# Five buffers for the later modulations' rows, and paired row chunks in the second product, of a two-layer decoder trunk

## The chip, the cores and the metric

One core of a Trainium2 chip runs the whole program. The metric is the device time of one execution in microseconds (us); the kernel before took 2310.33 us (median of three runs, 2307.93 to 2311.91). The engines are named as the profile names them: PE multiplies matrices, DVE (vector) and ACT (scalar) work on tiles, POOL (GpSimd) does a little arithmetic and issues transfers, SP only issues transfers. Each engine takes its instructions strictly in the order of the program.

## The reference

```python
for i in range(DEPTH):                       # 2 layers, D=2048, 256 tokens
    shift, scale, gate = ada_ln(c, mix_mod_w[i], mix_mod_b[i])   # silu(c) @ w + b, in three parts
    h = rms_norm(x, mix_norm_g[i]) * (1.0 + scale) + shift
    y = conformer_conv_module(h, ...) if i == 0 else stick_breaking_mixer(h, ...)
    x = x + gate * y
    shift, scale, gate = ada_ln(c, ffn_mod_w[i], ffn_mod_b[i])
    h = rms_norm(x, ffn_norm_g[i]) * (1.0 + scale) + shift
    x = x + gate * conv_ffn(h, ...)          # up to 2 x 5632, conv of width 3, silu(gate) * value, down
return rms_norm(x, final_norm_g)
```

`conformer_conv_module` is a first product `pw1` (to 2 x 2048), a gated depthwise convolution of width 31, a layer norm and a second product `pw2` (2048 to 2048). Every matrix is read once from HBM. Besides the weights there are four modulation matrices (`mix` and `ffn` of each layer) of 2048 x 6144, of which only the product with one vector, silu(c), is wanted.

## The kernel before

All activations lie transposed, in 16 tiles of 128 features by 256 tokens. A product takes its weights in blocks of 128 x 128, eight blocks (512 KB) to a piece. A piece is loaded into `raw` (SP's queue, L225, six buffers), split by ACT into a rounded part `wh` (L243) and by DVE into the rest `wl` (L247), four buffers of each. For every block PE runs three matmuls of 128 x 256: L297 (`wh` by the high part of the activation), L298 (`wh` by its low part), L299 (`wl` by the high part). Loads run five pieces ahead of PE and splits three.

The products follow each other on PE: `pw1`, `pw2`, then of the first ffn `up00a`, `up00b`, `up01a`, `down00`, `up01b`, `down01` (up and down in two halves each), attention, and the second ffn (`up10a` to `down11`). In the profile below `pw2` stands at 286.5 to 408.9 us, `up00b` at 433.1 to 658.0, `down00` at 669.2 to 793.3, `down01` at 1028.5 to 1163.5 and `down11` at 2175.7 to 2301.3. `down00`, `down01` and `down11` have 1056 matmuls each.

Whenever an output tile of `pw2` or of `down01` is complete, ACT or DVE adds it to the residual `x` (L942, L984), ACT squares it into `t` (L392), POOL adds the square to `sumsq` (L396), and ACT and DVE make the raw input of the next product from it (`hh` L448, `hl` L449).

The modulation vectors are made beside the products, in two ways:

- Row chunks. A 1 MB piece of the matrix is loaded with its input features on the partitions, and PE multiplies it by the vector `hot` in four matmuls of 128 x 512 (L576; each leaves two records). The bias columns of the conv module and the scale and half the shift of the first ffn come so. When a vector is complete, PE turns it (L592) and DVE adds the bias (L598). `load_rows` loads a chunk (L556, POOL's queue in `pw2`) as soon as its home is free: an `mraw` tile ("m") or, late, the one `zrow` tile ("z").
- Tiles. 1 MB with 128 outputs on the partitions is loaded into `mraw`, and DVE multiplies it by silu(c) and sums along the row (L330). Half of the first ffn's shift (eight tiles, `mod_part`, loaded on SP's queue among the weights) and all later vectors (112 tiles, `mods1`, loaded on POOL's queue by L323) come so. `mraw` has three buffers.

`mods0` and `mods1` are generators. After each piece a product adds its entry in `RATES` to a credit, and each whole credit advances the current generator by one step: one row chunk, or one tile loaded and, once more than two are ahead, the oldest one reduced. `behind(on)` keeps a tile's load behind the last POOL instruction written so far, and its reduction behind the last DVE instruction. The rest of the order on each engine is set by a scheduler.

Of the kernel before, what the change touches and what calls it, by code (L numbers as in the profile page):

```python
# [10 lines left out]
F32 = mybir.dt.float32  # L11
# [5 lines left out]
P = 128  # L17
# [14 lines left out]
MORE_ROWS = 4  # L32
SPLIT_ROWS = 3
# [2 lines left out]
ROWS_AT = {**{c: (11,) for c in (2, 4, 6, 8, 10, 12)}, 13: (16, 17), 14: (8, 12, 16), 15: (2, 13, 15, 17)}  # L36
ROWS_TAIL = 5

RATES = {"pw2": (1.0, 0.0), "up": (0.44, 0.25), "down": (0.5, 0.0), "qk": (0.3, 0.0), "v": (0.3, 0.0),
         "o": (0.45, -3.0), "up00a": (0.0, 0.0), "qk0a": (0.0, 0.0),  # L40
         "up00b": (0.44, -1.5), "up10a": (0.0, 0.0), "up10b": (0.25, -2.0), "v0": (0.0, 0.0), "qk0b": (0.3, -1.5)}
QUIET = 6
PRIORITY = 100


def plan(nbs, kts, first, stagger=4):
# [70 lines left out]
def hybrid_trunk(ctx: ExitStack, tc: tile.TileContext, cfg: Cfg, io: dict):  # L117
    nc = tc.nc
    D, T, H = cfg.D, cfg.T, cfg.H
    KD, KF, CW, FW = cfg.KD, cfg.KF, cfg.CW, cfg.FW  # L120
# [45 lines left out]
    cpar = {}  # L166
# [10 lines left out]
    fill = []  # L177
# [37 lines left out]
    def drain(gens):  # L215
        while gens:
            advance(gens, 1)
# [97 lines left out]
    macc = const.tile([P, 3 * KD], F32, name="macc")  # L315
    moda, have, shift_ready = {}, set(), {}

    def mod_load(m, nb, own=False):

        v = mpool.tile([P, D], F32, name="mraw")  # L320
        src = io["mt_" + m][mt_at[m].index(nb) if m in mt_at else nb]
        if own:
            nc.gpsimd.dma_start(v, src)  # L323
        else:
            load(src, v)
        return v

    def mod_reduce(m, nb, v):

        nc.vector.tensor_tensor_reduce(out=v, in0=v, in1=csr, scale=1.0, scalar=0.0, op0=ALU.mult, op1=ALU.add,  # L330
                                       accum_out=macc[:, nb:nb + 1])
# [11 lines left out]
    def mod_part(m, part, first):  # L343
        ahead = []
        for nb in range(part * KD + first, (part + 1) * KD):
            ahead.append((nb, mod_load(m, nb)))
            if len(ahead) > 1:
                mod_reduce(m, *ahead.pop(0))
            yield
        mod_reduce(m, *ahead.pop(0))  # L350
        mod_sum(m, part * KD + first, KD - first)
        yield

    later = []

# [139 lines left out]
    with ExitStack() as cv:  # L495
# [39 lines left out]
        def load_rows(most=1):  # L535

            while row_chunks and most:
                n = nrow["n"]
                near = n < nrow["near"]
                home = row_homes[n] if near else ("zmm"[n % 3] if n < 8 * KD // 4 else "zm"[n % 2]) if "z" in cpar else "m"  # L540
                cap = {"m": 3 if near else 1 + (n < 8 * KD // 4), "r": MORE_ROWS, "w": SPLIT_ROWS, "z": 1}[home]
                if sum(t[1] == home for t in row_tiles) >= cap:
                    break
                m, c, k0 = row_chunks.pop(0)
                src = io["mr_" + m][mr_at[m].index(c), :, k0 * 512:(k0 + 4) * 512]
                if home == "w":
                    v = [w_pool.tile([P, PW], F32R, name=x).bitcast(F32) for x in ("wh", "wl")]
                    for i in range(2):
                        load(src[:, i * PW:(i + 1) * PW], v[i])
                    v = [v[g // 2][:, g % 2 * 512:(g % 2 + 1) * 512] for g in range(4)]  # L550
                else:
                    v = (cpool2.tile([P, 4 * 512], F32, name="mrow", bufs=MORE_ROWS) if home == "r" else
                         cpar["z"].tile([P, 4 * 512], F32, name="zrow") if home == "z" else
                         mpool.tile([P, 4 * 512], F32, name="mraw"))
                    if "z" in cpar:
                        nc.gpsimd.dma_start(v, src)  # L556
                    else:
                        load(src, v)
                    v = [v[:, g * 512:(g + 1) * 512] for g in range(4)]
                row_tiles.append((v, home))  # L560
                nrow["n"] += 1
                most -= 1

        def mod_rows():

            for m, c0, n, done in rows_of:
                ps = (psum_acc if m == "ffn0" and c0 else psum_a)() if n else None  # L570
                for i in range(n):
                    for k0 in range(0, KD, 4):
                        v = row_tiles.pop(0)[0]
                        first, last = i == 0 and k0 == 0, i == n - 1 and k0 + 4 >= KD
                        for g in range(4):
                            nc.tensor.matmul(ps[32 * g:32 * g + 32, :], hot[:, k0 + g, 31 - i:63 - i],  # L576
                                             v[g], start=first, stop=last,
                                             tile_position=(0, 32 * g))
                        load_rows()
                        if later and nrow["bias"]:  # L580
                            later.pop(0)()
                        if last:
                            rows = cpool.tile([P, 512], F32, name="rows")
                            nc.scalar.copy(rows, ps)
                        else:
                            yield
                if n:
                    ps2 = psum_b()

                    def turn(rows=rows, n=n, ps2=ps2):  # L590
                        for b in range(4):
                            nc.tensor.matmul(ps2[:, b * n:(b + 1) * n], rows[:, b * P:(b + 1) * P], sel[:, :n],  # L592
                                             start=True, stop=True)

                    def bias(m=m, c0=c0, n=n, ps2=ps2, done=done):
                        o = modv[m][:, c0 * 4:(c0 + n) * 4].rearrange("p (c b) -> p b c", b=4)
                        v = pc(bname[m], c0 * 4, n * 4).rearrange("p (c b) -> p b c", b=4)
                        nc.vector.tensor_tensor(o, ps2[:, :4 * n].rearrange("p (b c) -> p b c", b=4), v, op=ALU.add)  # L598
                        done()

                    later.extend([turn, bias])
                    yield
            while later:
                later.pop(0)()
                yield

        def mods0():
            part = mod_part("ffn0", 0, 4 * cfg.rows0) if cfg.rows0 * 4 < KD else iter(())
            for _ in mod_rows():
                yield  # L610
                if ("ffn0", 1) in have and next(part, "end") != "end":
                    yield
            yield from part
            have.add(("ffn0", 0))

        gb = cpool.tile([P, KD], F32, name="gb")
        ready = {"k": 0}
        ys = [cpool.tile([P, T], F32, name=f"y{j}") for j in range(KD)]
        for kt in range(KD):
            nc.gpsimd.tensor_tensor(ys[kt], xs[kt], rs, op=ALU.mult)  # L620
        htiles = [h_tiles(kt) for kt in range(KD)]
# [328 lines left out]
    def ffn(i, entry, out):  # L950
        m = f"ffn{i}"
        NG = KF // 2 + 1
        with ExitStack() as fs:
            gpool = fs.enter_context(tc.tile_pool(name=f"g{i}", bufs=1))
            gh, gl = [None] * KF, [None] * KF
            pend = {}

# [24 lines left out]
            def down_done(h):  # L982
                def done(nb, ps):
                    nc.vector.scalar_tensor_tensor(xs[nb], ps[:, :T], gate(m, nb), xs[nb],  # L984
                                                   op0=ALU.mult, op1=ALU.add)
                    if h == 1 and i == 0:
                        out.add(nb)
                    elif h == 1:
                        out.add(xs[nb])
                        nc.scalar.activation(xs[nb], xs[nb], AF.Copy, scale=pc("fin_g", nb, 1))  # L990
                return done
# [6 lines left out]
            gemm(f"up{i}1b", hh, hl, up_done)  # L998
            act_tables("sqrt_and_others")
            gemm(f"down{i}1", gh, gl, down_done(1), quiet=QUIET)  # L1000

    def mods1():

        ahead = []

        def finish():
            m, part, nb, v = ahead.pop(0)
            on = last_of(nc.vector.engine)
            mod_reduce(m, nb, v)
            behind(on)  # L1010
            if nb + 1 == (part + 1) * KD:
                mod_sum(m, part * KD, KD)
                if part == 1:
                    mod_scale(m, 0, KD)
                have.add((m, part))

        for m, part in (("ffn0", 2), ("mix1", 1), ("mix1", 0), ("mix1", 2), ("ffn1", 1), ("ffn1", 0), ("ffn1", 2)):
            for nb in range(part * KD, (part + 1) * KD):
                on = last_of(nc.gpsimd.engine)
                ahead.append((m, part, nb, mod_load(m, nb, own=True)))  # L1020
                behind(on)
                if len(ahead) > 2:
                    finish()
                yield
        while ahead:
            finish()
            yield

    fill.append(mods1())
    entry1 = Entry("mix1")  # L1030
    ffn(0, entry, entry1)
# [268 lines left out]
```

## Time and profile before

| | |
|---|---|
| median of three runs | 2310.33 us (2307.93 to 2311.91) |
| the profiled execution | 2314.76 us, span 2313.1 us |
| mean granted clock of PE | 0.997 |
| busy: PE, DVE, ACT, POOL | 2273.3, 1737.9, 1163.5, 334.4 us |
| HBM read | 598.58 MB |

All times below are from the profiled execution, which is 4.43 us above the median of the runs. A busy PE is not a PE at its peak, since a matmul that waits inside the pipe counts as busy: stages are best compared by their length and the number of their matmuls. In a timeline row the bracket holds the idle time before the instruction and what ended it.

### The profile page before, as it was taken

What the parts mean: (1) busy time and instruction counts of PE and PEld (TensorE: products, weight loads), DVE (VectorE), ACT (ScalarE), POOL (GpSimd) and SP (SyncE); (2) the same over time, 40 slices, a digit from 0 to 9 for tenths busy, and PEclk for the clock granted to TensorE, in tenths of its full rate; (3) what the DMA queues carried; (4) which work ended last, traced back from release to release, by engine and by line L of the source; (5) the groups of instructions that cost most, each with busy time, mean ns of one, the idle gap of its engine ahead of it and who ended that gap; (6) DMA issues with size and microseconds to landing.
All of it is one profiled execution on the core that took longest, in us unless ns stands there. A gap on an engine that the chain in (4) does not pass through costs nothing.

```text
span 2313.1 us, 44241 instructions
## 1 busy us (share of the span) xinstructions
PE 2273.3 (98%) x17834; PEld 2170.2 (94%) x17834; DVE 1737.9 (75%) x2386; ACT 1163.5 (50%) x1776; POOL 334.4 (14%) x478
## 2 busy tenths in 40 slices
PE   7999999999999999999999999999999999999997
PEld 5888678999999999999999999999999999999997
DVE  7689968899998899998875555668666545666554
ACT  2056655755543355554465555647555434555543
POOL 4058713200001000001211000121000000000010
PEclk9999999999999999999999999999999999999999
DMA  9988798689999999998854555555555555555553
GB/s 394 417 323 308 272 370 350 236 319 362 344 362 386 361 343 358 348 357 329 330 182 164 165 172 174 164 191 177 189 191 186 189 187 187 190 186 190 188 186 110
DMA packets 139167, 603.56 MB, mean 261 GB/s; under 512 B 15441, under 2 KB 15569, under 8 KB 115153
## 3 DMA queue, kind: packets, MB, share of 16 engines
q1 hardware_dynamic: 120242, 464.42, 56.0%
q0 software_dynamic: 18720, 136.32, 15.8%
q8 instruction: 139, 2.28, 0.4%
q14 instruction: 66, 0.54, 0.1%
HBM read 598.58 MB, written 2.10 MB: 260 GB/s over the span
## 4 chain that ended last, share of the span: by engine, by line
PE 62%; issue 23%; DVE 5%; DMA 5%; POOL 2%; ACT 1%; POOLq 0%; SPq 0%; DVEq 0%; ACTq 0%
PE ps L297 17%; PE ps L298 17%; PE ps L299 16%; PE ps L663 5%; DMA mraw<-in_mt_mix 3%; POOL mraw L323 2%; DVE mraw L330 2%; DMA mraw<-in_mt_ffn 2%; DVE wl L247 1%; PE ps L1125 1%; PE ps L1127 1%; PE ps L1126 1%; PE ps L576 1%; PE auxa L576 1%; ACT hl L712 0%
## 5 line engine op out<-in xcount | busy, mean ns | idle before, releaser
L247 DVE TENSOR_TENSOR wl<-raw,wh 128x1024 fp32r<-128x1024 f32 x688 | 844.4, 1231 | 414.7 <-ACT wh L243 409.1
L243 ACT CAST wh<-raw 128x1024 fp32r<-128x1024 f32 x688 | 719.3, 1048 | 822.9 <-PE ps L298 645.9
L297 PE MATMUL ps<-hh,wh 128*128 128x256 f32 (+1 forms) x3264 | 915.8, 281 | 0.0
L298 PE MATMUL ps<-hl,wh 128*128 128x256 f32 (+1 forms) x3264 | 912.1, 279 | 0.0
L299 PE MATMUL ps<-hh,wl 128*128 128x256 f32 (+1 forms) x3264 | 908.3, 278 | 0.1
L298 PEld LDWEIGHTS ps<-hl,wh 128*128 128x128 f32 x3264 | 617.7, 189 | 0.3
L299 PEld LDWEIGHTS ps<-hh,wl 128*128 128x128 f32 x3264 | 612.8, 188 | 0.7 <-DVE wl L247 0.7
L297 PEld LDWEIGHTS ps<-hh,wh 128*128 128x128 f32 x3264 | 612.7, 188 | 0.3
L299 PE MATMUL ps<-gh,wl 128*128 128x256 f32 x1408 | 394.6, 280 | 7.1 <-DVE wl L247 7.1
L298 PE MATMUL ps<-gl,wh 128*128 128x256 f32 x1408 | 396.4, 282 | 0.0
L297 PE MATMUL ps<-gh,wh 128*128 128x256 f32 x1408 | 395.4, 281 | 0.0
L330 DVE CUSTOM_DVE_ANT_0 mraw<-mraw,csr 128x2048 f32<-128x2048 f32 x152 | 348.5, 2294 | 52.6 <-DMA mraw<-in_mt_mix 30.9
L299 PEld LDWEIGHTS ps<-gh,wl 128*128 128x128 f32 x1408 | 266.0, 189 | 8.1 <-DVE wl L247 8.1
L298 PEld LDWEIGHTS ps<-gl,wh 128*128 128x128 f32 x1408 | 266.9, 190 | 0.0
L297 PEld LDWEIGHTS ps<-gh,wh 128*128 128x128 f32 x1408 | 266.2, 189 | 0.0
L396 POOL TENSOR_TENSOR sumsq<-sumsq,t 128x256 f32<-128x256 f32 x56 | 65.0, 1162 | 885.8 <-ACT t L392 885.6
L663 PE MATMUL ps<-hh,raw 128*128 128x256 f32 x832 | 188.8, 382 | 0.0
L663 PEld LDWEIGHTS ps<-hh,raw 128*128 128x128 f32 x832 | 157.8, 191 | 28.3 <-issue 6.7
L964 DVE SCALAR_TENSOR_TENSOR t<-ps,par,t 128x254 f32<-128x254 f32 x328 | 157.1, 479 | 3.9
L703 DVE SCALAR_TENSOR_TENSOR auxb<-u,cpar,auxb 128x256 f32<-128x256 f32 x297 | 121.6, 483 | 4.5 <-ACT auxb L687 3.7
L838 POOL TENSOR_TENSOR y<-y,hl 128x256 f32<-128x256 f32 x143 | 104.4, 730 | 13.4 <-ACT hl L712 3.3
L961 ACT ACTIVATE t<-ps,par 128x256 f32<-128x256 f32 x164 | 91.8, 560 | 0.0
(247 smaller groups left out, 2271.3 us busy)
## 6 DMA issues: line engine op xcount, KB each, us to landing
raw<-in_w_down SPq DMA_DIRECT2D x176, 512.0 KB, 3.8
mraw<-in_mt_ffn POOLq DMA_DIRECT2D x64, 1024.0 KB, 8.3
raw<-in_w_pw SPq DMA_DIRECT2D x96, 512.0 KB, 7.9
mraw<-in_mt_mix POOLq DMA_DIRECT2D x48, 1024.0 KB, 8.1
raw<-in_w_up01b SPq DMA_DIRECT2D x84, 512.0 KB, 6.8
raw<-in_w_up11b SPq DMA_DIRECT2D x84, 512.0 KB, 3.5
raw<-in_w_up00b SPq DMA_DIRECT2D x80, 512.0 KB, 6.5
raw<-in_w_up10b SPq DMA_DIRECT2D x80, 512.0 KB, 3.5
```

What stands on the lines that cost most here:

```text
L243: nc.scalar.copy(wh[:, :n], v[:, :n])
L247: nc.vector.tensor_tensor(wl[:, :n], v[:, :n], wh[:, :n].bitcast(F32), op=ALU.subtract)
L297: nc.tensor.matmul(o, wh[:, c], xh[kt], start=first, stop=False, skip_group_check=halves > 0)
L298: nc.tensor.matmul(o, wh[:, c], xl[kt], start=False, stop=False, skip_group_check=halves > 0)
L299: nc.tensor.matmul(o, wl[:, c], xh[kt], start=False, stop=left[nb] == 0, skip_group_check=halves > 0)
L330: nc.vector.tensor_tensor_reduce(out=v, in0=v, in1=csr, scale=1.0, scalar=0.0, op0=ALU.mult, op1=ALU.add, accum_out=macc[:, nb:nb + 1])
L396: engine.tensor_tensor(self.sum, self.sum, sq, op=ALU.add)
L663: nc.tensor.matmul(banks[j][:, nb // KD * T:(nb // KD + 1) * T], w[:, b * P:(b + 1) * P], hf[kt], start=first, stop=left[j] == 0, skip_gro ...
L703: nc.vector.scalar_tensor_tensor(conv_ps[j], us[j % UBUFS][:, k:k + T], tap(j, k), conv_ps[j], op0=ALU.mult, op1=ALU.add)
L838: nc.gpsimd.tensor_tensor(ys[c], ys[c], pr, op=ALU.add)
L961: nc.scalar.activation(y, ps[:, :T], AF.Identity, bias=pc(f"fdb{i}", nb, 1), scale=w(FW - 1))
L964: nc.vector.scalar_tensor_tensor(y[:, s:], ps[:, :T - s], w(k), y[:, s:], op0=ALU.mult, op1=ALU.add)
```

## The change

The change has three parts. `mods1` gets a ring of five buffers, three `mraw` of the old pool and two of a new pool opened in the first ffn, and reduces a tile once five are ahead, so that four loads lead; the rate of `up00b` goes from 0.44 (credit from -1.5) to 0.45 (credit from 0), and what is left is drained at the end of the ffn. In `pw2` each step of `mods0` takes two row chunks, and their homes follow a written list, in which "y" stands for two tiles `yhalf` that before held the first product's sixteen `y` tiles and are dead by then; the caps on homes change to match. The eight tiles of the first ffn's shift go from SP's queue to POOL's, with two loads ahead in place of one.

```diff
+LATE_HOMES = "mmzyymmzyymzyyzyyzyy"
...
-         "up00b": (0.44, -1.5), "up10a": (0.0, 0.0), "up10b": (0.25, -2.0), "v0": (0.0, 0.0), "qk0b": (0.3, -1.5)}
+         "up00b": (0.45, 0.0), "up10a": (0.0, 0.0), "up10b": (0.25, -2.0), "v0": (0.0, 0.0), "qk0b": (0.3, -1.5)}
+MORE_MODS = 2
...
     def mod_part(m, part, first):
         ahead = []
         for nb in range(part * KD + first, (part + 1) * KD):
-            ahead.append((nb, mod_load(m, nb)))
-            if len(ahead) > 1:
+            ahead.append((nb, mod_load(m, nb, own=True)))
+            if len(ahead) > 2:
                 mod_reduce(m, *ahead.pop(0))
+                yield
+        while ahead:
+            mod_reduce(m, *ahead.pop(0))
             yield
-        mod_reduce(m, *ahead.pop(0))
         mod_sum(m, part * KD + first, KD - first)
...
-                home = row_homes[n] if near else ("zmm"[n % 3] if n < 8 * KD // 4 else "zm"[n % 2]) if "z" in cpar else "m"
-                cap = {"m": 3 if near else 1 + (n < 8 * KD // 4), "r": MORE_ROWS, "w": SPLIT_ROWS, "z": 1}[home]
+                home = row_homes[n] if near else LATE_HOMES[n - nrow["near"]] if "z" in cpar else "m"
+                cap = {"m": 3 if near else 2, "r": MORE_ROWS, "w": SPLIT_ROWS, "z": 1, "y": 2}[home]
...
+                         cpool.tile([P, 4 * 512], F32, name="yhalf", bufs=2) if home == "y" else
...
-                        load_rows()
+                        load_rows(2 if nrow["bias"] else 1)
...
         def mods0():
+
             part = mod_part("ffn0", 0, 4 * cfg.rows0) if cfg.rows0 * 4 < KD else iter(())
-            for _ in mod_rows():
+            rows = mod_rows()
+            while next(rows, "end") != "end":
+                if nrow["bias"]:
+                    next(rows, "end")
+                    yield
+                    for _ in range(2 if ("ffn0", 1) in have else 0):
+                        next(part, "end")
+                        yield
                 yield
-                if ("ffn0", 1) in have and next(part, "end") != "end":
-                    yield
-            yield from part
+            for _ in part:
+                yield
+                yield
             have.add(("ffn0", 0))
...
-        ys = [cpool.tile([P, T], F32, name=f"y{j}") for j in range(KD)]
+        yhalf = [cpool.tile([P, KD // 2 * T], F32, name="yhalf", bufs=2) for _ in range(2)]
+        ys = [yhalf[j * 2 // KD][:, j % (KD // 2) * T:(j % (KD // 2) + 1) * T] for j in range(KD)]
...
+            if i == 0:
+                more["pool"] = fs.enter_context(tc.tile_pool(name="mods", bufs=MORE_MODS))
...
             gemm(f"down{i}1", gh, gl, down_done(1), quiet=QUIET)
+            drain(fill)
 
     def mods1():
 
-        ahead = []
+        ahead, ring = [], [mpool] * 3 + [more["pool"]] * MORE_MODS
...
-                ahead.append((m, part, nb, mod_load(m, nb, own=True)))
+                ahead.append((m, part, nb, mod_load(m, nb, own=True, pool=ring[0])))
+                ring.append(ring.pop(0))
                 behind(on)
-                if len(ahead) > 2:
+                if len(ahead) == len(ring):
                     finish()
```

The first place is POOL in `pw2`. Before, the row chunks (`mr`, one matrix row piece each) go to `mraw` and `zrow` in turn:

```order
L556 DMA mraw<-in_mr_ffn 128x2048 x4
L556 DMA zrow<-in_mr_ffn 128x2048
L556 DMA mraw<-in_mr_ffn 128x2048 x2
L556 DMA zrow<-in_mr_ffn 128x2048
L556 DMA mraw<-in_mr_ffn 128x2048
L556 DMA zrow<-in_mr_ffn 128x2048
L556 DMA mraw<-in_mr_ffn 128x2048
L556 DMA zrow<-in_mr_ffn 128x2048
L396 TENSOR_TENSOR sumsq<-sumsq,t 128x256 x4
```

After the change, from the fifth chunk in `pw2` on (`mt` is a tile of the shift, which SP loaded before):

```order
L561 DMA yhalf<-in_mr_ffn 128x2048 x3
L561 DMA zrow<-in_mr_ffn 128x2048
L561 DMA yhalf<-in_mr_ffn 128x2048 x3
L561 DMA zrow<-in_mr_ffn 128x2048
L561 DMA yhalf<-in_mr_ffn 128x2048
L400 TENSOR_TENSOR sumsq<-sumsq,t 128x256
L561 DMA yhalf<-in_mr_ffn 128x2048
L400 TENSOR_TENSOR sumsq<-sumsq,t 128x256
L326 DMA mraw<-in_mt_ffn 128x2048
```

Ten late chunks now go through the two `yhalf` tiles, and the first four of these use the same tile one after the other. The eight tiles of the shift stand behind sums on POOL (the next seven likewise).

The second place is DVE in `down01`, with the buffers' numbers. Before, the reduction of `mraw_12652` (the load that waits for the sum of the square of this `x`) stands three `wl` pieces behind it:

```order
L984 SCALAR_TENSOR_TENSOR x_82<-ps_12502,v_ffn0_99,x_82 128x256
L247 TENSOR_TENSOR wl_12584<-raw_12518,wh_12583 128x1024
L449 SCALAR_TENSOR_TENSOR hl10_12598<-x_82,a_mix1_7037,hh10_12597 128x256
L247 TENSOR_TENSOR wl_12625<-raw_12548,wh_12624 128x1024
L330 ISA mraw_12515,macc_102<-mraw_12515,csr_83 128x2048
L330 ISA macc_102 128x1
L247 TENSOR_TENSOR wl_12658<-raw_12581,wh_12657 128x1024
L330 ISA mraw_12652,macc_102<-mraw_12652,csr_83 128x2048
```

After, seven of twelve such reductions stand eight to ten pieces behind the `x` that releases their load (before, thirteen stood three to seven behind), but `mraw_12223`, loaded after the sum of the square of this `x`, is reduced ahead of the older `mraw_12075` and `mraw_12149`:

```order
L1000 SCALAR_TENSOR_TENSOR x_82<-ps_12106,v_ffn0_99,x_82 128x256
L250 TENSOR_TENSOR wl_12185<-raw_12119,wh_12184 128x1024
L453 SCALAR_TENSOR_TENSOR hl6_12199<-x_82,a_mix1_7030,hh6_12198 128x256
L464 TENSOR_TENSOR hl14_12971<-v_mix1_100,hh14_12970 128x2
L464 TENSOR_TENSOR hl15_13059<-v_mix1_100,hh15_13058 128x2
L250 TENSOR_TENSOR wl_12229<-raw_12152,wh_12228 128x1024
L250 TENSOR_TENSOR wl_12259<-raw_12182,wh_12258 128x1024
L333 ISA mraw_12223,macc_102<-mraw_12223,csr_83 128x2048
```

The order has moved here by one reduction fewer in the stage, and the ring lets a tile wait longer before it is reduced; three more loads stand in front of `down01` (97 steps of the generator in place of 94). On PE the order in `pw2` changes in the grouping of the row chunks only: 14 groups between the product's matmuls in place of 23.

More of the change, by code (lines that the diff above doesn't have):

```diff
@@ L316, in hybrid_trunk, with mod_load @@
     moda, have, shift_ready = {}, set(), {}
-    def mod_load(m, nb, own=False):
-        v = mpool.tile([P, D], F32, name="mraw")
+    def mod_load(m, nb, own=False, pool=None):
+        v = (pool or mpool).tile([P, D], F32, name="mraw")
         src = io["mt_" + m][mt_at[m].index(nb) if m in mt_at else nb]
@@ L608, in mods0 @@
             part = mod_part("ffn0", 0, 4 * cfg.rows0) if cfg.rows0 * 4 < KD else iter(())
-            for _ in mod_rows():
+            rows = mod_rows()
[6 more added lines that the diff above has]
+                        yield
                 yield
-                if ("ffn0", 1) in have and next(part, "end") != "end":
-                    yield
-            yield from part
+            for _ in part:
+                yield
+                yield
             have.add(("ffn0", 0))
@@ L1027, in mods1 @@
             yield
+    more = {}
     fill.append(mods1())
```

## The prediction

> **What bounds the kernel now.** I read the page's busy shares first, then lengths of stages in windows, then the waits and the timeline of the stages that are too long.
>
> ```profile
> PE 2273.3 (98%) x17834; PEld 2170.2 (94%) x17834; DVE 1737.9 (75%) x2386; ACT 1163.5 (50%) x1776; POOL 334.4 (14%) x478
> ...
> 669.20:793.30 124.10, 124.10 (x1057) 124.10 (x1057) 109.63 (x111) 47.41 (x47) 12.18 (x23) 1.00 0.97 376
> 1028.50:1163.50 135.00, 127.94 (x1058) 126.93 (x1057) 118.37 (x134) 58.29 (x80) 25.18 (x33) 0.97 0.85 322
> 2175.70:2301.30 125.60, 124.94 (x1061) 124.52 (x1060) 58.72 (x61) 57.89 (x77) 13.07 (x14) 1.00 0.46 152
> ```
>
> PE is busy for 98%, so only time that it loses can be won. The rows are `down00`, `down01` and `down11`: stretch, length, then busy time and count of PE, PEld, DVE, ACT and POOL, granted clock, share of the DMA engines, GB/s. With the same 1056 matmuls `down00` takes 124.1 us and `down01` 135.0: 10.9 us are lost there. The waits of `down01` (total, times, longest) say by whom, first on PE, then on DVE, and PE's row shows the longest:
>
> ```profile
> PE ps L299 <- DVE wl L247: 7.1, 5, 4.0
> ...
> DVE mraw L330 <- DMA mraw<-in_mt_ffn: 11.9, 8, 4.1
> ...
> 1138.55 0.58 PE L299 MATMUL ps<-gh,wl 128*128 128x256 f32 x1 [4.00 <-DVE wl L247]
> ...
> 1137.40:1144.30 6.90, 5.75 (x27) 5.75 (x28) 6.90 (x8) 3.65 (x5) 1.57 (x2) 0.51 0.65 225
> ```
>
> PE waits 7.1 us for `wl`, and DVE, which makes it, waits 11.9 us for tiles of the modulation. After the 4.0 us wait the granted clock is 0.51 for 6.9 us, so about 6.9 x 0.49 = 3.4 us more are lost; 7.1 + 3.4 = 10.5, nearly the 10.9. The Trainium skill, "TensorE: Matmul & The Clock Gate", section "HAM oscillation — how this bites in real kernels", says that the clock halves after gaps of over about 3.4 us; the trace agrees with its one gap of 4.0 us. Where the long wait comes from is seen on DVE, then on POOL, then in that load's landing time:
>
> ```profile
> 1122.69 0.47 DVE L984 SCALAR_TENSOR_TENSOR x<-ps,v_ffn,x 128x256 f32<-128x256 f32 x1
> 1123.09 1.21 DVE L247 TENSOR_TENSOR wl<-raw,wh 128x1024 fp32r<-128x1024 f32 x1
> ...
> 1127.10 2.29 DVE L330 CUSTOM_DVE_ANT_0 mraw<-mraw,csr 128x2048 f32<-128x2048 f32 x1 [0.78 <-DMA mraw<-in_mt_ffn]
> ...
> 1134.66 2.29 DVE L330 CUSTOM_DVE_ANT_0 mraw<-mraw,csr 128x2048 f32<-128x2048 f32 x1 [4.12 <-DMA mraw<-in_mt_ffn]
> ...
> 1123.83 1.07 POOL L396 TENSOR_TENSOR sumsq<-sumsq,t 128x256 f32<-128x256 f32 x1 [4.84 <-ACT t L392]
> 1124.85 0.57 POOL L323 DMA_DIRECT2D mraw<-in_mt_ffn  x1
> ...
> mraw<-in_mt_ffn POOLq DMA_DIRECT2D x1, 1024.0 KB, 9.8
> ...
> mraw<-in_mt_ffn POOLq DMA_DIRECT2D x1, 1024.0 KB, 5.9
> ...
> 1051.97 2.29 DVE L330 CUSTOM_DVE_ANT_0 mraw<-mraw,csr 128x2048 f32<-128x2048 f32 x1 [3.21 <-DMA mraw<-in_mt_ffn]
> ```
>
> The load sits on POOL behind the sum for the `x` of 1122.69. It is issued at 1124.85 and lands 9.8 us later, 12 us after that `x`; DVE gets to the reduction after 7.9 us of work and shorter waits, and stands. The last two rows, for later, are the quickest such load of the stage (issued at 1094.20) and DVE's first long wait in it.
>
> **The ring and the rate.** The number of reductions is the same, and the order shows one fewer in `down01` (2.29 us of DVE). `up00b` gets about one more; DVE there has room for it:
>
> ```profile
> 433.10:658.00 224.90, 224.52 (x1923) 224.31 (x1922) 215.19 (x287) 121.45 (x174) 15.90 (x30) 1.00 0.91 339
> ```
>
> 224.9 - 215.2 = 9.7 us are idle, and PE has no wait of DVE's making there, so I cost this at nothing; if that cover is gone, it is 2.3 us at most. Loads issued earlier in `up00b` ride on a DMA share of 0.91. Three fewer remain for `down01`, where the share is 0.85.
>
> In `down01` most reductions now stand eight to ten `wl` pieces behind their release. A piece of PE is 24 matmuls, 24 x 124.1/1056 = 2.8 us, so eight pieces are 22 us, twice the 12 us needed: these do not wait. But the scheduler lets the newest tile overtake, at a lead of three, three or four times. Three pieces are 8.4 us at PE's pace against 12: a wait of 3.6 us each, up to 7 where DVE is late already and does the work at once. The first such wait costs PE little, since DVE starts with up to three pieces in hand, and the 3.2 us wait at the stage's begin is gone. I put PE's remaining waits at 4.4 us, without a drop of the clock: 10.9 - 4.4 = 6.5 us won. The ends are 11 (no waits left) and 1.5 (waits as before, less one reduction).
>
> **The second product.** Its rows are PE's row chunks (busy, mean), PE at one of them, the only wait, DVE's waits for the shift's tiles, and the loads:
>
> ```profile
> L576 PE MATMUL ps<-mraw,hot 128*32 128x512 f32 x71 | 11.2, 604 | 0.0
> L576 PE MATMUL auxa<-zrow,hot 128*32 128x512 f32 x32 | 5.3, 605 | 0.0
> ...
> 342.55 1.07 PE L576 MATMUL auxa<-zrow,hot 128*32 128x512 f32 x8
> 343.55 0.38 PE L297 MATMUL ps<-zh,wh 128*128 128x256 f32 x1
> 343.77 0.28 PE L298 MATMUL ps<-zl,wh 128*128 128x256 f32 x1
> 343.88 0.28 PE L299 MATMUL ps<-zh,wl 128*128 128x256 f32 x1
> ...
> PE ps L297 <- ACT t L941: 2.1, 2, 1.6
> ...
> DVE mraw L330 <- DMA mraw<-in_mt_ffn: 9.7, 4, 4.0
> ...
> 344.05 0.53 POOL L556 DMA_DIRECT2D zrow<-in_mr_ffn  x1 [6.10 <-PE auxa L576]
> ...
> mraw<-in_mr_ffn POOLq DMA_DIRECT2D x10, 1024.0 KB, 8.2
> ...
> mraw<-in_mr_ffn POOLq DMA_DIRECT2D x1, 1024.0 KB, 5.2
> ```
>
> Pairing: a chunk takes 1.0 us of PE either way. Leaving it, the first matmul takes 343.77 - 343.55 = 0.22 us in place of 0.12; entering costs about the same, so a group costs 0.2 us, and 14 groups in place of 23 save 1.8 us (0 to 3).
>
> The "y" chunks: the first four go through one tile, each load waiting until PE has read the one before, as the `zrow` row shows it for its single tile ("<-PE auxa L576"). Between two of these reads the order puts some 44 matmuls and a chunk or less, or 20 matmuls and three chunks: 5.5 to 5.8 us of PE. A load takes 0.5 us of issue and 5.2 us at its quickest, 8.2 in the median, so each link makes PE wait 0 to 3 us. I take 0.75, nearer to the quick row, because fewer row loads are in flight together: 4 x 0.75 = 3.0 us (0 to 12). The Trainium skill, "DMA: Bandwidth & Descriptors", section "Anatomy of one DMA — SWDGE (gpsimd) path", gives 2.0 us plus the bytes at 436 GB/s, an estimate of 4.4 us for 1 MB, by which no link would wait and the sum would be 3 us lower; no load here was as quick as that, and the measurement decides.
>
> The shift's tiles: SP's queue loses eight loads between weights, so `raw` comes sooner, but no PE wait is put down to `raw`: nothing. On POOL the eight loads now stand behind `sumsq`, as in `down01`, and what is queued behind them are the remaining row chunks and sums. Their reductions come close behind the first output tiles, whose run of 84 matmuls is no longer broken by row chunks. Rows of DVE and the same rows' waits:
>
> ```profile
> L247 DVE TENSOR_TENSOR wl<-raw,wh 128x1024 fp32r<-128x1024 f32 x34 | 42.2, 1251 | 9.8 <-ACT wh L243 9.8
> L330 DVE CUSTOM_DVE_ANT_0 mraw<-mraw,csr 128x2048 f32<-128x2048 f32 x8 | 18.3, 2287 | 9.7 <-DMA mraw<-in_mt_ffn 9.7
> L449 DVE SCALAR_TENSOR_TENSOR hl<-x,a_ffn,hh 128x256 fp32r<-128x256 f32 x15 | 11.2, 749 | 2.6 <-ACT hh L448 2.6
> L942 DVE TENSOR_TENSOR x<-x,t 128x256 f32<-128x256 f32 x15 | 6.2, 416 | 0.0
> ```
>
> An output tile costs DVE 0.42 + 0.75 and half a piece, 0.63: 1.8 us, while PE makes one in 12 matmuls, 1.4 us. Eight of them put DVE 3.2 us behind, three reductions 6.9 more, and a wait for the first load some 3.5 (as long as the longest, 4.0, of before): 13.6 us, against three pieces in hand, 8.4, and two chunks of PE, 2. That leaves 3 us of waiting (0 to 8), in place of the 2.1 of before. Together: -1.8 + 3.0 + 3.0 - 2.1 = +2.1 us (-5 to +15).
>
> **Sum.** -6.5 + 2.1 = -4.4 us on the profiled execution, 2314.76 to 2310.3. That execution was 4.4 us above the median; I carry the difference over unchanged: 2310.33 - 4.4 = 2305.9 us.
>
> **Rivals.**
> - All of `down01` comes back and `pw2` stays level: the spare lead swallows the overtaking tiles too. For it speaks that a load can land in 5.9 us. 2310.33 - 10.9 = 2299.4.
> - The overtaking tiles hold DVE as before, one of them over 4 us, and the clock drops again: only the reduction that left (2.3 us) is won, and `pw2` gives it back: 2310.33 - 2.3 + 2.1 = 2310.1. For it: the order's leads of three, against 12 us from `x` to landing.
> - Slower: the single "y" tile. If each link takes the median landing, four links cost 4 x 3.0 = 12 us, and one wait over 4 us a clock drop of 3.4: `pw2` +14.5, and the sum +8.0, 2318.3. It decides for slower from links of 2.4 us on without the drop (the sum is then past zero). Against it: before, PE never waited for the single `zrow` tile.
>
> **Chances.** 0.2% (4.6 us) is what a measurement tells from no change: under 2305.7 is faster, over 2314.9 slower. Forecast (2301 to 2310) 0.46, half of it on each side of 2305.7, a little more below: 0.25 faster, 0.21 same. Full recovery 0.19, faster. No change in `down01` 0.20: 0.18 same, 0.02 slower. The "y" tile 0.15: 0.03 same, 0.12 slower. Together 0.44, 0.42, 0.14. The range 2298 to 2315 leaves out a tenth above and less below.
>
> **What the profile would show.** `down01` at 128 to 129 us with clock 1.00, and DVE's waits for `mraw` there under 8 us, each behind a tile that overtook. In `pw2`, waits of PE at L581 (the row chunks) for loads into `yhalf`: under 1 us each right, 3 us the slower rival. `pw2` at 124 to 125 us in all, with 3 us of waits for `wl` or banks around the first outputs. `up00b` still at 225 us, else the rate was not free. Wrong would be the whole argument if `down01` lost time with no wait of DVE for a tile.

## The result, and the profile after

The changed kernel took 2318.98 us (median of five runs, 2316.23 to 2321.09) against 2310.33 us: the ratio is 1.0039, with a 95% interval of 1.0028 to 1.0050. It is 8.7 us slower, and above the forecast range. Its profiled execution took 2321.09 us, with a span of 2319.4 us.

All the time went in one stage, and the other gave some back. These are the windows of `pw2` and of `down01` after the change (length, then busy time and count of PE, PEld, DVE, ACT, POOL, then PE's granted clock, DMA share and GB/s); before they were 122.4 and 135.0 us long.

```profile
285.60:419.00 133.40, 121.65 (x952) 101.08 (x952) 92.58 (x146) 69.32 (x127) 27.73 (x38) 0.96 0.87 328
1038.60:1169.70 131.10, 127.57 (x1058) 126.95 (x1057) 118.85 (x137) 58.93 (x80) 23.37 (x31) 0.97 0.85 314
```

`pw2` grew by 11.0 us, `down01` shrank by 3.9, and no stage behind `pw2` but `down01` moved by more than 0.1 us; what runs ahead of `pw2` was 0.9 us shorter in this execution (`pw2` begins at 285.6 us in place of 286.5). PE's waits in `pw2` of the changed kernel are these:

```profile
PE ps L581 <- DMA yhalf<-in_mr_ffn: 6.2, 3, 4.1
PE auxa L581 <- DMA yhalf<-in_mr_ffn: 3.5, 1, 3.5
PE ps L302 <- DVE wl L250: 2.0, 2, 1.6
```

9.7 us are waits for row chunks in `yhalf`, where before PE had waited 2.1 us in all and never for a chunk. The first wait is the longest. PE's row, POOL's two rows, the row of DVE that POOL waited for, and the load's landing time show how it comes about:

```profile
316.00 1.94 PE L581 MATMUL ps<-yhalf,hot 128*32 128x512 f32 x8 [4.09 <-DMA yhalf<-in_mr_ffn]
...
306.52 0.53 POOL L561 DMA_DIRECT2D yhalf<-in_mr_ffn  x1 [5.92 <-DVE t L937]
318.26 0.53 POOL L561 DMA_DIRECT2D yhalf<-in_mr_ffn  x1 [11.22 <-PE ps L581]
...
305.80 0.42 DVE L937 TENSOR_TENSOR t<-yhalf,rstd 128x256 f32<-128x256 f32 x1
...
yhalf<-in_mr_ffn POOLq DMA_DIRECT2D x1, 1024.0 KB, 9.4
...
331.29 0.64 PE L581 MATMUL ps<-yhalf,hot 128*32 128x512 f32 x4 [0.44 <-DMA yhalf<-in_mr_ffn]
339.64 0.64 PE L581 MATMUL ps<-yhalf,hot 128*32 128x512 f32 x4 [1.65 <-DMA yhalf<-in_mr_ffn]
```

The tile still held the first product's `y`. DVE reads the last of the eight `y` tiles in it at 305.80, between pieces of `wl`. POOL waits for that with the load at the head of its queue, issues it at 306.52, and it lands 9.4 us later; PE has stood for 4.09 us by then. The next load wants the same tile, so POOL waits until PE has read the chunk, 11.2 us, and nothing behind it on POOL can start. The chunks that follow through the same tile cost PE little: the last two rows, 0.44 and 1.65 us, are all its waits for them. Two windows show what follows, and one pair (before, then after) shows the DMA engines over the same 40 us:

```profile
316.00:321.00 5.00, 5.00 (x22) 3.34 (x23) 0.81 (x3) 0.00 (x0) 0.53 (x1) 0.50 0.56 186
396.10:399.50 3.40, 3.40 (x18) 2.19 (x11) 1.11 (x2) 0.58 (x1) 0.00 (x0) 0.50 1.03 422
...
300.00:340.00 40.00, 40.00 (x320) 30.62 (x314) 27.73 (x47) 22.09 (x36) 4.76 (x9) 1.00 1.00 400
...
300.00:340.00 40.00, 33.82 (x263) 27.74 (x265) 24.12 (x43) 19.16 (x33) 3.71 (x7) 0.91 0.83 311
```

After the 4.09 us gap the clock is 0.50 for 5 us, and again for 3.4 us from 396.1 on: some 2.5 and 1.7 us more of PE. Before, these 40 us ran at a DMA share of 1.00 and PE did 320 instructions; after, the share is 0.83 and PE did 263. The second drop follows a gap of its own, at the last pair of chunks. PE's row, and POOL's rows of the load it waits for, which lands 8.7 us after its issue:

```profile
395.75 1.63 PE L581 MATMUL auxa<-yhalf,hot 128*32 128x512 f32 x8 [3.53 <-DMA yhalf<-in_mr_ffn]
...
385.92 1.13 POOL L400 TENSOR_TENSOR sumsq<-sumsq,t 128x256 f32<-128x256 f32 x1 [6.32 <-ACT t L396]
387.00 0.57 POOL L561 DMA_DIRECT2D yhalf<-in_mr_ffn  x1
```

This load stood behind a sum that itself waited 6.32 us for ACT. The sum by waits: 9.7 + 2.0 + 4.2 of clock, less the 2.1 us of before, is 13.8. The 2.8 us beyond the measured 11.0 are not accounted for; what fewer groups save may be in them, but it was not measured apart.

In `down01` the tile shown in the section on the change, `mraw_12223`, is the one that hurts. POOL's rows, DVE's row of its reduction, PE's wait behind it, the window after that, and DVE's waits of the stage:

```profile
1100.24 1.12 POOL L400 TENSOR_TENSOR sumsq<-sumsq,t 128x256 f32<-128x256 f32 x1 [7.46 <-ACT t L396]
1101.31 0.57 POOL L326 DMA_DIRECT2D mraw<-in_mt_ffn  x1
...
1109.82 2.29 DVE L333 CUSTOM_DVE_ANT_0 mraw<-mraw,csr 128x2048 f32<-128x2048 f32 x1 [5.77 <-DMA mraw<-in_mt_ffn]
...
1113.71 0.58 PE L302 MATMUL ps<-gh,wl 128*128 128x256 f32 x1 [2.90 <-DVE wl L250]
...
1113.80:1119.80 6.00, 6.00 (x28) 6.00 (x29) 6.00 (x7) 2.77 (x4) 1.48 (x3) 0.50 0.84 310
...
DVE mraw L333 <- DMA mraw<-in_mt_ffn: 8.5, 3, 5.8
```

Issued at 1101.31, reduced as soon as it landed at 1109.82, while two older tiles, landed by 1099.1, stood behind it on DVE. It cost a wait of 5.77 us on DVE, 2.90 on PE, and 6 us at half clock.

### The profile page after: what moved, and what is told of

It reads as the page before. It is cut to its first block, busy times and chain, and to the rows that moved or that the text cites. A ratio compares the mean times of both kernels' runs of the same rounds, so it can differ in the third digit from the quotient of the medians.

```text
span 2319.4 us, 44237 instructions
## 1 busy us (share of the span) xinstructions
PE 2274.1 (98%) x17834; PEld 2173.1 (94%) x17834; DVE 1736.3 (75%) x2386; ACT 1165.6 (50%) x1776; POOL 334.0 (14%) x486
## 4 chain that ended last, share of the span: by engine, by line
PE 85%; DVE 6%; DMA 6%; issue 2%; ACT 1%; POOL 0%; DVEq 0%; SPq 0%; POOLq 0%; ACTq 0%
PE ps L300 24%; PE ps L301 24%; PE ps L302 24%; PE ps L677 5%; DMA mraw<-in_mt_mix 3%; DVE mraw L333 2%; DMA yhalf<-in_mr_ffn 2%; DVE wl L250 1%; DMA mraw<-in_mt_ffn 1%; PE ps L1144 1%; PE ps L1145 1%; PE ps L1146 1%; PE ps L581 1%; PE auxa L581 0%; DVE hl L385 0%
## 5 line engine op out<-in xcount | busy, mean ns | idle before, releaser
L852 POOL TENSOR_TENSOR yhalf<-yhalf,hl 128x256 f32<-128x256 f32 x143 | 104.4, 730 | 13.4 <-ACT hl L726 3.3
```

What stands on the lines that cost most here:

```text
L852: nc.gpsimd.tensor_tensor(ys[c], ys[c], pr, op=ALU.add)
```

## The experiments

Times are medians of the runs; a ratio is to the kernel before, run beside it on the same chip. That took 2309.1 us for the first four kernels below; 2309.3 for pairs alone, `yhalf` without pairs, `yhalf` later and the order with the ring; 2309.0 for the first `yhalf` chunk elsewhere; and 2311.5 for the last three. Times are compared by their distance to it. For `pw2` I give the length in the profiled execution, and how much of it is not the 768 matmuls at 0.118 us, ahead of the second turn (L592, when the scale is complete) and behind it. Before: 122.4 us, 16.5 ahead, 15.2 behind. The changed kernel: 133.4, 23.5 and 19.3. These lengths are of one execution each.

**The ring alone.** The kernel before with `ring`, `MORE_MODS`, the rate of `up00b` and the last `drain`.

```diff
-        ahead = []
+        ahead, ring = [], [mpool] * 3 + [more["pool"]] * MORE_MODS
...
-                if len(ahead) > 2:
+                if len(ahead) == len(ring):
```

> The kernel before with the ring of five buffers, the rate of up00b and the drain alone; pw2 as before. Theory Y (the time was lost in pw2 on the one yhalf tile) and theory S (it was lost in pw2 because the shift's eight tiles went to POOL's queue, behind sums) agree here: pw2 122.4 us as before, down01 131 us in place of 135, in all 4 us faster than before (2306). If the ring itself costs time anywhere else (up00b's rate), the gain is under 2 us.

Measured: 2306.83 us, ratio 0.9990 (0.9981 to 0.9999). `down01` was 128.1 us, with 7.1 us of DVE's waits for tiles, and `up00b` 224.8 as before. The ring gives 2.2 us, about half of the 4 us expected. Two lengths say why. In `pw2` the order on every engine is that of before, and yet it took 124.1 us here: a stage's length differs by as much as 1.7 us from execution to execution. In `down01` the two kernels after this one (the row chunks alone, the shift alone) have the order of before on every engine. Their rows:

```profile
1041.70:1171.60 129.90, 125.14 (x1059) 124.33 (x1058) 117.92 (x134) 58.52 (x80) 25.22 (x33) 1.00 0.88 335
...
1031.20:1161.40 130.20, 125.06 (x1058) 124.25 (x1057) 117.83 (x134) 58.32 (x80) 25.20 (x33) 1.00 0.87 333
```

They took 129.9 and 130.2 us at a clock of 1.00, where the profile of before shows 135.0 with a clock drop. So, as far as three executions show, that profile caught a bad one of this stage. From 130 to the 128.1 of the ring is 2 us, as the medians say.

**The row chunks alone.** The changed kernel without the ring, and with the shift's tiles on SP's queue.

```diff
-            ahead.append((nb, mod_load(m, nb, own=True)))
+            ahead.append((nb, mod_load(m, nb)))
```

> The row chunks in pairs from five places alone, the shift's tiles on SP's queue, no ring. Theory Y: PE waits for yhalf loads as in the changed kernel, about 9.7 us, and the clock drops once: pw2 131 to 134 us, 9 to 11 us slower than before. Theory S: without the shift on POOL the waits for yhalf are at most half of that, pw2 under 127 us, under 5 us slower.

Measured: 2324.06 us, ratio 1.0063 (1.0049 to 1.0076); `pw2` 136.2 us, 29.1 ahead of the turn and 16.5 behind it, with 10.6 us of waits for `yhalf`. It is 15.0 us slower than before, more than theory Y's 9 to 11. Theory Y holds for the half ahead of the turn, and moving the shift to POOL does not cause these waits.

**The shift on POOL alone.** The kernel before with `own=True` and two loads ahead in `mod_part`.

> The shift's eight tiles on POOL's queue with two ahead alone; row chunks one by one into mraw and zrow as before, no ring. Theory Y: pw2 within 2 us of 122.4, no change. Theory S: DVE waits more for these tiles, PE for wl, pw2 126 us or more, at least 4 us slower than before.

Measured: 2312.83 us, ratio 1.0013 (1.0004 to 1.0022); `pw2` 125.6 us, 16.5 ahead and 18.5 behind. A cost of 3 to 4 us (3.2 by the stage, 3.8 by the medians), between the two theories, and all behind the turn: the first half is as before.

**No `yhalf`.** The changed kernel with another list.

```diff
-LATE_HOMES = "mmzyymmzyymzyyzyyzyy"
+LATE_HOMES = "mmzmmzmmzmmzmmzmmzmm"
```

> The changed kernel with the late row chunks in mraw and zrow tiles only (the list of homes is mmz over and over), pairs, shift on POOL and ring kept. Theory Y: the waits at the row chunks go (under 2 us left), pw2 122 to 124 us, down01 131, the whole about 4 us faster than before and 12 faster than the changed kernel. Theory S: pw2 stays at 128 or more, since the tiles of the shift still stand behind sums on POOL.

Measured: 2316.43 us, ratio 1.0028 (1.0016 to 1.0039). Neither theory alone: ahead of the turn 17.7, almost the 16.5 of before, so there `yhalf` was the cost; behind it 22.2, more than with `yhalf`. There PE waited 4.4 us for one chunk in `mraw` and 2.3 us for a bank (where it adds up its results, and from which ACT had still to read), and the clock fell to half at each. `pw2` 130.5 us.

**Pairs alone.** The same list, the shift on SP's queue, the ring kept.

> Row chunks in pairs alone: homes mmz over and over, the shift's tiles on SP's queue, the ring kept. Theory P (pairing costs by itself, since two chunks are wanted at once while loads come at the pace of full DMA queues): pw2 127 us or more, with waits of PE for mraw or zrow. If pairing costs nothing and the 130.5 us of the kernel without yhalf came from the shift on POOL's queue alone: pw2 122 to 125 us, 3 us faster than before.

Measured: 2321.56 us, ratio 1.0056 (1.0040 to 1.0071); `pw2` 135.4 us, 17.9 ahead and 27.0 behind. Theory P is right on the size and wrong on the reason. Two windows behind the turn, SP's queue's waits from 335 to 385 us, and ACT's rows for two pieces of weights:

```profile
335.00:350.00 15.00, 15.00 (x118) 12.44 (x117) 5.79 (x10) 7.60 (x14) 2.53 (x4) 1.00 0.62 236
350.00:365.00 15.00, 11.73 (x79) 8.99 (x78) 10.84 (x13) 5.28 (x12) 4.63 (x4) 0.89 0.39 133
...
SPq L228 <- PE auxa L581: 23.5, 3, 9.5
SPq L228 <- DMA mraw<-in_mr_ffn: 11.4, 1, 11.4
...
372.06 1.04 ACT L246 CAST wh<-raw 128x1024 fp32r<-128x1024 f32 x1 [3.88 <-DMA raw<-in_w_pw]
375.84 1.05 ACT L246 CAST wh<-raw 128x1024 fp32r<-128x1024 f32 x1 [2.02 <-DMA raw<-in_w_pw]
```

The DMA engines are not full here: their share falls to 0.39. SP stands with a shift tile that wants an `mraw` buffer held by a row chunk, the weights queue behind it, and ACT then waits for `raw`. So the move of the shift to POOL, which costs 3 us alone, by these rows keeps the weights free when chunks are paired (22.2 behind the turn in place of 27.0).

**`yhalf` without pairs.** The list of the change, one chunk to a step, the old `mod_part`, the ring.

> The homes with yhalf alone: one row chunk to a step as before, the shift's tiles on SP's queue with one ahead, the ring kept. Theory Y (the single tile that is free late): PE waits for the first yhalf load (about 4 us, since its tile is free only when DVE has read the last of the old y tiles at about 306 us) and some more, pw2 128 us or more. Theory P: with single steps the loads are in time, pw2 under 125 us.

Measured: 2319.01 us, ratio 1.0042 (1.0029 to 1.0056); `pw2` 136.4 us, 27.3 ahead of the turn, 8.3 us of waits for `yhalf` with the longest 4.3. Theory Y again: the homes cost this without any pairing.

**`yhalf` later.** The changed kernel with one more list.

```diff
-LATE_HOMES = "mmzyymmzyymzyyzyyzyy"
+LATE_HOMES = "mmzmmzmmzyyzyyzyyzyy"
```

> The changed kernel with the yhalf homes from the tenth late chunk on only (mmz three times ahead of it, then yyz), so that the first yhalf load comes when its tile is long free and both tiles are used. Theory Y: the early waits for yhalf go; what is left is what the kernel without yhalf showed, pw2 about 130 us, or less where two more places help: 126 to 130. If the yhalf waits had nothing to do with when the tile is free, pw2 stays at 133.

Measured: 2309.66 us, ratio 0.9999 (0.9990 to 1.0008); `pw2` 125.6 us, 23.9 ahead of the turn and only 11.2 behind it. The length is at the edge of what theory Y expected, but not for its reason: ahead of the turn PE still waited 6.0 us for `yhalf`. In this list four tiles of the shift, not none, are issued ahead of the sums on POOL; their loads stand in the first half (DMA share 1.00 from 300 to 340 us) and no longer in the second.

**The first `yhalf` chunk elsewhere.** The changed kernel with one letter changed.

```diff
-LATE_HOMES = "mmzyymmzyymzyyzyyzyy"
+LATE_HOMES = "mmzmymmzyymzyyzyyzyy"
```

> The changed kernel with one home of the list changed: the fourth late chunk goes to mraw in place of yhalf (mmzmymmzyymzyyzyyzyy). Its load needs not wait for the last reading of the old y tiles. If that wait (the tile is free at 306 us, the load lands at 316) is what makes PE's first stop of 4.1 us and the drop of the clock after it, the first half of pw2, up to the turn, gets 5 to 7 us shorter and the time falls to 2312 to 2314. If the loads of this half are late because the DMA engines are full, the stop moves to another chunk and the time stays within 2 us of the changed kernel's 2319.

Measured: 2310.61 us, ratio 1.0008 (0.9999 to 1.0018): 1.6 us above before, where the changed kernel is 8.7 above. The stop was not removed, it moved to the next chunk (3.9 us of waiting, since that one now goes first to the same tile); the first half gained 3.2 us (20.3), and the second 6.2 (13.1), with two tiles of the shift issued ahead of the sums. The expectation failed on both counts and on the time.

**Reductions in order, with the ring.** The ring alone, and each reduction also kept behind the one before.

```diff
+        done = []
...
             mod_reduce(m, nb, v)
             behind(on)
+            if done:
+                behind(done.pop())
+            done.append(list(nc.cur_bb.bb.instructions)[-1])
```

> The ring alone (the kernel of the first experiment) with each reduction of a tile also kept behind the reduction of the tile before it, so that no tile overtakes. If the overtaking tiles cause what down01 still loses (128.1 us against 124.2 in down00), DVE's waits for tiles there fall to under 1 us and down01 to 124 to 126 us, 2 to 4 us less than the ring alone, 2303 to 2304.5. If the loads are too late for another reason (the DMA queues), DVE waits as long as with the ring alone and the time stays at 2306.8.

Measured: 2302.36 us, ratio 0.9970 (0.9960 to 0.9981); `down01` 124.0 us, the length of `down00`, and no wait of DVE for a tile in it.

**Reductions in order, without the ring.** The kernel before with these lines alone.

> The kernel before with only the reductions kept in order, three buffers and the old rate. If both are needed (the lead of the ring and the order), DVE still waits for tiles in down01, 8 us or more, since a tile stands three to six pieces behind its release in any order, and the time is within 2 us of before. If the order alone does it, down01 falls to under 127 us and the time to 2303 to 2305.

Measured: 2303.03 us, ratio 0.9963 (0.9951 to 0.9976). The order alone does it, against the first branch of the expectation. DVE's order differs from before at two places, where a newer tile had stood ahead of an older one (`mraw_11716` ahead of `mraw_11653`, `mraw_12652` ahead of `mraw_12578`); these were the waits of 3.21 and 4.12 us. The stage's length and DVE's waits are to be set against 130 to 135 us and 8 to 12 us in the three kernels with the order of before. `down01` and DVE's waits in it, with three buffers:

```profile
1028.40:1152.40 124.00, 124.00 (x1058) 124.00 (x1057) 117.86 (x134) 60.22 (x80) 25.44 (x33) 1.00 0.92 350
...
DVE mraw L330 <- DMA mraw<-in_mt_ffn: 0.9, 2, 0.5
```

Two pairs of reductions put back in order took DVE's waits from 11.9 to 0.9 us, so nearly all of the shorter waits went with the two long ones. I read it so that a late tile also holds its buffer, and with it each later load; that was not tested apart. The changed kernel has seven such overtakings.

**The changed kernel with reductions in order.**

> The changed kernel with the reductions in order and nothing else. pw2 stays at 133 us with its waits for yhalf, down01 goes from 131.1 to 124 to 125: 2312 to 2314.5 us, that is 2 to 5 us slower than before, if the two stages do not depend on each other.

Measured: 2312.23 us, ratio 1.0003 (0.9993 to 1.0012); `pw2` 131.4 us, `down01` 124.0. It is 0.7 us slower than before, where 2 to 5 were expected. `pw2` stays long when `down01` is mended, so the one did not cause the other.

**Both repairs.** Reductions in order, and `yhalf` from the thirteenth late chunk on, its two tiles in turn.

```diff
-LATE_HOMES = "mmzyymmzyymzyyzyyzyy"
+LATE_HOMES = "mmzmmzmmzmmzyyzyyzyy"
```

> The changed kernel with two repairs: reductions in order, and the list of homes mmzmmzmmzmmzyyzyyzyy, so that yhalf is used from the thirteenth late chunk on and its two tiles in turn; pairs, shift on POOL and the ring kept. If the late single tile and the overtaking were all that was wrong, PE waits for yhalf under 2 us, pw2 takes 119 to 123 us, down01 124, in all 2299 to 2303, as fast as the ring with the order alone or faster. If pairing costs by itself (theory P), pw2 is 125 us or more and the time 2305 or more.

Measured: 2306.69 us, ratio 0.9980 (0.9971 to 0.9989); `down01` 124.0, but `pw2` 129.7 us: no waits for `yhalf`, 4.9 us for `zrow` and 3.8 us for a bank. The expectation's second branch came true: the late tile and the overtaking were not all that was wrong. It is faster than before and slower than the order alone. In no form tried was the new `pw2` shorter than the old one: 124.0 to 136.4 us, against 122.4 to 124.1 with the old order.

The version that beats both kernels is the kernel before with its reductions in order, without or with the ring: 2303.03 and 2302.36 us, 8.5 and 7.0 us below before.

## Why the prediction was wrong

- *What bounds the kernel.* Right: PE's lost time is where the time moves, `down01` lost it to DVE's waits for tiles, and in that execution the long one halved the clock. The 3.4 us for the drop count 1.15 us of the wait twice: in the 6.9 us of that row PE ran for 5.75, so the drop cost some 2.9.
- *The ring: 6.5 us won in `down01`.* Right in sign, mis-sized: 3.9 us between the two profiles, 2.2 us by the medians with the ring alone. The term that was too large is the 10.9 us to be won: the same order took 129.9 and 130.2 us in two other kernels, so mostly some 6 were there. What I left for the overtaking tiles, 4.4 us without a drop of the clock, is what the ring alone shows (128.1 us at a clock of 1.00); in the changed kernel they cost 3.5 us of waits and 3.0 of clock (6 us at 0.50). The reduction fewer, read from the order, was not there either: the traces have 21 in `down01` after the change and 20 before. And the step behind the term failed. I took the short lead for the cause and the overtaking for a remainder; the experiments show the overtaking as the cause, before the change already: with the order mended, three buffers take 124.0 us, the length of `down00`.
- *The rate of `up00b` at nothing.* Right: 224.9 us before and after.
- *Pairing saves 1.8 us by fewer groups.* The saving was not measured apart. That pairing costs behind the turn (27.0 us against 15.2 when it is alone, with the shift on SP's queue) was missing from the sum.
- *The "y" chunks: four links of 0.75 us, 3.0 us.* This is the step that failed most. The waits were 9.7 us, and the clock dropped twice, 4.2 us. The links themselves were not the trouble: behind the first load they cost 0.44 + 1.65 = 2.1 us. The sum had nothing for the rest: 4.1 us for the first load, which waits for DVE's last reading of the old `y`; 3.5 us for the last one, which stood behind a sum on POOL; and the clock after both. I priced only the chain of loads behind the first one, and not when the tile comes free for that. That the 9.7 us lie inside my bound of 12 is luck, since the bound was worked out for the links.
- *The shift's tiles on POOL, 3 us in place of 2.1.* Mis-sized: a net cost of 0.9 us was forecast, and alone it cost 3.2 (125.6 us of `pw2` against 122.4, all behind the turn), with 3.5 us of PE's waits for a bank and 1.7 for a chunk in `zrow`. In the changed kernel the term is about right: 2.0 us of waits for `wl` are seen.
- *The carry to the median.* Wrong: the changed kernel's profiled execution was 2.1 us above its median, not 4.4. Before, the excess of 4.4 us is near the 5 us by which `down01` with 135.0 us lies above the 130 of the two other executions; then the sum counted as gain what the median does not lose, though with three executions this is not proved. Roughly, of the 13.1 us between forecast and measured, 8.9 are `pw2` (11.0 where 2.1 was forecast) and 4.3 the ring (2.2 where 6.5 was forecast).
- *The rivals.* The slower one gave 2318.3 us and had 0.15; 2318.98 was measured. That the number is so near is partly luck, since it has 6.5 us for the ring and 14.5 for `pw2`. Its mechanism is half right: late `yhalf` loads and a dropped clock, but by one load that could not start and one behind a sum, not by four equal links. Its argument against itself, that PE had never waited for the single `zrow` tile, did not carry over: `zrow` was free when it was wanted. Its limit of 2.4 us a link does not follow from the sum either: that passes zero at 1.85 us a link, and the edge of slower at 3.0.
- *What the profile would show.* Waits at L581 of up to 4.1 us were the sign named for the slower rival, and they stand there. `pw2` took 133.4 us for 124 to 125. `down01` at 128 to 129 us with a clock of 1.00 and under 8 us of DVE's waits is what the ring alone shows; the changed kernel had 131.1 us, 0.97 and 8.5.

What stays open: why the half of `pw2` behind the turn is 11.2 us in one list and 22.2 in another was followed only in the kernel of pairs alone. In the others it goes with how many tiles of the shift are issued ahead of the sums (four: 11.2, two: 13.1, none: 19.3 and 22.2), but the kernel with both repairs, with three ahead, has 17.5, and the shift alone, with two, 18.5, so this is not shown as the cause.

## What to carry to other kernels

A buffer taken over from dead data is free when its last reader has run in that engine's queue, not when the algorithm is done with it: find that instruction in the trace and add the load's landing time before counting it as a place. One load that waits at the head of an in-order queue stops all loads behind it (here POOL stood for 11.2 us), so one more home can go with a lower DMA share (1.00 before and 0.83 after, over the same 40 us). Before buying buffers for a late load, look whether the consumer takes them in the order in which they were loaded; here one dependency per reduction was worth 8 us, and these runs show nothing that the two extra buffers add to it. And look at a stage in more than one execution before you price what can be won in it: a wait that drops the clock in one execution can be shorter, and drop nothing, in the next (here 4.00 and 2.69 us behind the same tile, before and with the shift alone).

## What the runs showed of the hardware

- The clock fell to half after a PE wait of 2.90 us in `down01`, for 6 us, and after waits of 4.09 and 3.53 us in `pw2`, for 5 and 3.4 us; a wait of 1.65 us did not do it. Between these there is no sharp limit in these traces: of two waits of 2.69 us in `down01`, the one in the kernel with `yhalf` without pairs was followed by 3.4 us at 0.51, and the one in the kernel with the shift alone by none. The Trainium skill, "TensorE: Matmul & The Clock Gate", section "HAM oscillation — how this bites in real kernels", names gaps of over about 3.4 us; the gap of 2.90 us was enough here, and the measurement decides.
- The same 1 MB row load landed in 5.1 us at the quickest in the changed kernel and in 12.6 and 14.8 us with the DMA share at 1.00 (the kernel with `yhalf` later): a spread of nearly three that the median of 8.2 us before the change does not show. The quick one ran while the DMA share was 0.59 (318.2 to 323.4 us). The Trainium skill's "DMA: Bandwidth & Descriptors", section "Anatomy of one DMA — SWDGE (gpsimd) path", gives an estimate of 4.4 us; every 1 MB row load in these traces took longer.
